# A two-layer decoder trunk on one core: values and gates in three passes, chunk products by fours, output gates in alternating banks, modulation transposes within a block, scores of 128 columns

## Chip, cores and metric

The kernel runs on one core of a Trainium2 chip. The time is the device time of one execution in microseconds (us), as the median of several runs. TensorE (PE) does the matrix products, VectorE (DVE) and ScalarE (ACT) the elementwise work, GpSimd (POOL) some fills and sums, and SyncE (SP) starts most of the transfers.

## The reference

1024 tokens of 1024 numbers, all in 32-bit floats, go through two layers. Layer 0 mixes tokens with an mLSTM of 8 heads (q and k 64 wide, v 128 wide, chunks of 128 tokens) and has a squared-ReLU MLP of 4096. Its result gives keys and values for causal attention with a low-rank latent and a rotary part in layer 1, which has an MLP as well. Around each part stand norms whose gains and shifts (the modulation) are computed from a condition vector by products with matrices of 1024 x 6144.

```python
proj = h @ w_in                       # 1024 x 3088: q 512, k 512, v 1024, i 8, f 8, og 1024
q, k, v, ig, fg, og = jnp.split(proj, splits, axis=-1)
# per chunk of 128 tokens and head; ib = input gate, bb = running sum of log sigmoid(forget gate)
log_d = bb[..., :, None] - bb[..., None, :] + ib[..., None, :]      # causal part only
m_t = jnp.maximum(bb + m, jnp.max(log_d, axis=-1))
s = (q @ k.T) * exp(log_d - m_t)                  # scores times decay
num = exp(bb + m - m_t) * (q @ C) + s @ v         # C: the state, 64 x 128 per head
h = num / jnp.maximum(jnp.abs(den), exp(-m_t))    # den: the same with a column of ones for v
C = decay * C + (w * k).T @ v
y = (rmsnorm(h) * jax.nn.sigmoid(og)) @ w_out
...
x = x + g1 * rmsnorm(y);  h = modulate(rmsnorm(x), sh2, sc2);  x = x + g2 * rmsnorm(sqrelu_mlp(h))
```

## The kernel before

**Products.** A 32-bit number is written as a rounded high part and a rounded rest (hi and lo). `mm3` (L230 to L234) computes one product as three rounded ones: lo by hi (L232), hi by lo (L233), hi by hi (L234). Weights come by `wload` (L204, L211 for the transfer): SP brings 768 or 1024 columns into one of four `raw` buffers, ScalarE rounds them to hi (L189), VectorE subtracts (L190) and gives lo. Both parts stand in `ws`, eight buffers. `prompt` gives such work priority over the rest.

**Banks.** Results lie in PSUM: two tiles `ps` of one bank (512 columns of 32 bits), two `pc` of one bank, and two `pm` of two banks each.

**Tokens** go through in two halves of 512, `hfs[0]` and `hfs[1]`. For each half the mLSTM part is written as generators, and each `yield` ends a step:

- `qk_in` (the second half) and `qk_pairs` (the first): q and k with features on the partitions, from 24 products of 512 columns for each group of 128 features.
- `gates_in` (L626): the 16 gate columns of `w_in` are loaded, split, and set into a weight of 128 columns per block of 128 inputs. 16 pairs of products of 512 columns (L642, L643) give the gates with the gates on the partitions, in a `ps` bank `gp`. `gates0` (L702 to L751) then makes the decay terms on 8 partitions by a chain on VectorE and ScalarE from L707 to L751; at its end stands `RM`, the maxima and weights that later products read. Twelve transposes (L756) give the same per token, in `gc`.
- `intra0` (L761), for each of four pairs of heads: the decay of two heads by two products each in a `pc` bank (L772 the mask, L775 reading `RM`) and four exponentials each (L779), eight score products of 64 rows in a `pm` tile (L787), the product of both (L792), and one product of `selW` with `RM` (L795) that scales q.
- `v_in` (L657): the values, with tokens on the partitions: four passes of 256 columns, each with two loads and for each block of 128 tokens 24 products of 256 columns, in a `ps` bank.
- `chunks0` (L814), for each chunk of 128 tokens: q with the state `Cst` (L831, 64 rows), the weighted scores `PT` with v (L836, 128 rows), transposes of k (L844), the new state (L879) and transposes of the result (L894), which are written over `PT`.
- `og0` (L690): the output gates, eight projections in `ps`, each with three activations (L695 to L697). `split_o` multiplies and splits them for `wout`, the projection after.

**Background.** `ada_chunk` (L348) computes the modulation: four transfers of two 512-column blocks into `raw` (L353), eight products on VectorE (L358, L360) that sum them into `tma`, two empty steps, then four transposes (L340) into a `pc` bank and a reduction (L342). 24 such chunks of both layers stand in `bg0` and `bg1`.

**What sets the order.** The generators are put together by hand: `with_bg(g, bg, n)` takes n background steps with each step of g, `weave` and `weave_n` take so many steps of a second generator with each of the first, `in_turn` runs three side by side. A scheduler then places what they issue by its own costs and priorities; each engine runs its instructions in the order that results. In the MLPs and the attention, `two_streams` (L2028) runs a dense generator (an MLP or a projection, whose steps report `"hid"` or `"within"`) with another, and takes background steps (`fill`) between them.

**Attention scores** (`score_mm`, L1506): for a block of 128 queries, the keys up to its end in groups of up to 512 columns, five products each and a mask (L1522). A group is at least 256 columns wide, even where only 128 of them are causal.

Of the kernel before, what the change touches and what calls it, by code (L numbers as in the profile page):

```python
# [82 lines left out]
def kernel(  # L83
# [542 lines left out]
    def gates_in(hf):  # L626
        h = hf.h
        wg = raw(F32R).rearrange("p (a b) -> p a b", b=P)
        nc.gpsimd.memset(wg.bitcast(F32), 0.0)
        rg = tmp()  # L630
        rgv = rg[:, :128].rearrange("p (k n) -> p k n", n=16)
        nc.sync.dma_start(rgv, wcols(w_in, 2048, 16))
        for g in range(2):
            s = ts(g, 8)
            nc.scalar.copy(wg[:, :, 32 * g : 32 * g + 8], rgv[:, :, s])
            nc.vector.tensor_sub(
                wg[:, :, 64 + 32 * g : 72 + 32 * g], rgv[:, :, s],
                wg[:, :, 32 * g : 32 * g + 8].bitcast(F32),
            )
        gp = ps()  # L640
        for k in range(KD):
            nc.tensor.matmul(gp, wg[:, k], h.lo[k], start=k == 0, stop=False)  # L642
            nc.tensor.matmul(gp, wg[:, k], h.hi[k], start=False, stop=k == KD - 1)  # L643
        hf.gp = gp
        yield from gates0(hf)
        yield
# [10 lines left out]
    def v_in(hf):  # L657
# [9 lines left out]
        for j in range(4):  # L667
            w0 = wload([(0, 0, wcols(w_in, 1024 + j * 256, 256, 0, 4))], 256)
            w1 = wload([(0, 0, wcols(w_in, 1024 + j * 256, 256, 4, 4))], 256)
            for t in range(4):  # L670
                pt = ps()[:, :256]
                for k in range(KD):
                    w = w0 if k < 4 else w1
                    mm3(
                        pt, h.hi[k][:, ts(t, P)], h.lo[k][:, ts(t, P)],
                        w[0][:, k % 4], w[1][:, k % 4], k == 0, k == KD - 1,
                    )
                i = pt.rearrange("p (a b) -> p a b", b=P)
                if j < 3:
                    parts = [(hf.v[t][8][:, 2 * j : 2 * j + 2, 0:128], i)]  # L680
                else:
                    parts = [(hf.v[t][6 + e][:, 0:128], i[:, e]) for e in range(2)]
                for o, a in parts:
                    if t % 2:
                        nc.vector.tensor_copy(o, a)
                    else:
                        nc.scalar.copy(o, a)
                yield
# [13 lines left out]
    def gates0(hf):  # L702
# [4 lines left out]
        nc.vector.tensor_copy(t1, gp[64:72])  # L707
        nc.vector.scalar_tensor_tensor(t1, gp[0:8], col(GB, 1)[0:8], t1, ALU.add, ALU.add)
        nc.vector.tensor_copy(t2, gp[96:104])
        nc.vector.tensor_copy(t3, gp[32:40])  # L710
        nc.vector.scalar_tensor_tensor(t2, t3, col(GB + 1, 1)[0:8], t2, ALU.add, ALU.add)
# [49 lines left out]
    def intra0(hf):  # L761
# [3 lines left out]
        for p_ in range(4):  # L765
# [18 lines left out]
            st = pm()  # L784
            for j in range(4):
                for r in range(2):
                    nc.tensor.matmul(  # L787
                        st[:, r, ts(j, P)], kp[ts(r, 64), ts(j, P)], qp[ts(r, 64), ts(j, P)],
                        start=True, stop=True,
                    )  # L790
            for r in range(2):
                nc.vector.tensor_mul(PT[:, r], st[:, r], E[r])  # L792
# [21 lines left out]
    def chunks0(hf):  # L814
# [4 lines left out]
        for j in range(4):  # L819
# [3 lines left out]
            nvs = []  # L823
            for q in range(2):
                num = pm()
                nv = num[:, :, 0 : 2 * VE].rearrange("p b (i e) -> p b i e", e=VE)
                for i in range(2):
                    p_ = 2 * q + i

                    for r in range(2 if g > 0 else 0):  # L830
# [1405 lines left out]
```

## Time and profile before

| | |
|---|---|
| median of 3 runs | 2370.01 us (2367.67 to 2371.02) |
| profiled execution | 2373.3 us, of which 2371.2 are the span from the first to the last instruction |
| TensorE busy | 2334.8 us, 98% of the span, 12197 products |
| weight loads of TensorE | 1967.3 us, 83%, beside the products |
| VectorE busy | 1605.2 us, 68% |
| ScalarE busy | 1099.8 us, 46% |
| GpSimd busy | 147.6 us, 6% |
| granted TensorE clock | 0.996 on average |
| transfers | 420.77 MB, 177 GB/s on average |

Stages by the timeline: the first half's values and intra products from 82 to 160 us, its chunks to about 225, the second half's projections, gates, intra products and values to about 326, its chunks to about 400, the second output gates to about 447. Attention scores stand between 972 and 1826 us, beside dense work.

How to read the lines: a timeline's row has the start in us, the duration, the engine, the line of the kernel, the operation, what it writes and reads, rows x columns of the weight tile, the shape, and in brackets the wait before it with what released it. A group's row has busy time and mean duration in ns behind the first bar, and the engine's idle time ahead of these instructions with its releasers behind the second. A window's row has the window's length and, for PE, the weight loads, VectorE, ScalarE and GpSimd, the busy time and number of instructions, then the granted clock, the busy share of the transfer engines and GB/s. Products overlap in a pipeline, so their durations add up to more than the time that passes.

### The profile page before, as it was taken

To read this page: it belongs to the slowest core of one execution; us is meant where nothing else is said; L and a number is where in the kernel's file an instruction comes from. 1 tells how busy PE (TensorE), PEld (TensorE's weight loads), DVE (VectorE), ACT (ScalarE), POOL (GpSimd) and SP (SyncE) were. 2 spreads that over 40 slices of the span, in tenths; PEclk is the share of its full clock that TensorE was granted. 3 is DMA by queue.
4 is the path that set the end of the run, shared out by engine and by line. 5 is a ranking of instruction groups with operands and counts; after the bars stand their busy time and mean duration, and the time that the engine had idled before them with its cause. 6 is when DMAs were issued, how large, how long until landed. Compare 5 with 4: busy or idle time off the path is not lost.

```text
span 2371.2 us, 32533 instructions
## 1 busy us (share of the span) xinstructions
PE 2334.8 (98%) x12197; PEld 1967.3 (83%) x12197; DVE 1605.2 (68%) x2657; ACT 1099.8 (46%) x1826; POOL 147.6 (6%) x345
## 2 busy tenths in 40 slices
PE   7999999999999999999999999999999999999998
PEld 5888888788888888888888888888888888989997
DVE  6667866868666677877774967766566478457556
ACT  4355334655333464434444544434434445655543
POOL 1000000000001210111110110001001000000000
PEclk9999999999999999999999999999999999999999
DMA  9453564544656966667754675885544552657552
GB/s 312 143 145 89 181 184 137 170 130 150 187 178 166 313 184 197 185 200 205 227 157 117 196 208 176 269 272 167 173 129 132 147 169 86 189 175 218 165 183 89
DMA packets 408350, 420.77 MB, mean 177 GB/s; under 512 B 27427, under 2 KB 310112, under 8 KB 404608
## 3 DMA queue, kind: packets, MB, share of 16 engines
q1 hardware_dynamic: 402272, 385.02, 51.9%
q0 software_dynamic: 5920, 33.66, 6.5%
q8 instruction: 96, 1.57, 0.3%
q14 instruction: 62, 0.51, 0.1%
HBM read 359.37 MB, written 92.80 MB: 191 GB/s over the span
## 4 chain that ended last, share of the span: by engine, by line
PE 90%; DVE 4%; DMA 3%; ACT 2%; issue 1%; SPq 0%; DVEq 0%; ACTq 0%
PE ps L232 16%; PE ps L233 15%; PE ps L234 15%; PE pm L232 10%; PE pm L233 10%; PE pm L234 10%; PE pc L234 2%; PE pc L232 2%; PE pc L233 2%; DMA raw<-in_mlp_w_dram 1%; PE pc L1637 1%; DMA raw<-in_a_w_in_dram 1%; DVE wl L190 1%; PE pm L836 1%; PE pm L1523 1%
## 5 line engine op out<-in xcount | busy, mean ns | idle before, releaser
L190 DVE TENSOR_TENSOR wl<-raw,wh 128x1024 fp32r<-128x1024 f32 (+2 forms) x382 | 458.5, 1203 | 385.8 <-ACT wh L189 281.4
L189 ACT CAST wh<-raw 128x1024 fp32r<-128x1024 f32 (+2 forms) x382 | 394.0, 1035 | 657.9 <-PE ps L232 241.8
L232 PE MATMUL ps<-k,wl 128*128 128x512 f32 (+1 forms) x1464 | 560.3, 383 | 2.6 <-ACT k L695 1.4
L234 PE MATMUL ps<-k,wh 128*128 128x512 f32 (+1 forms) x1464 | 551.6, 377 | 0.0
L233 PE MATMUL ps<-k,wh 128*128 128x512 f32 (+1 forms) x1464 | 550.7, 376 | 0.0
L232 PEld LDWEIGHTS ps<-k,wl 128*128 128x128 f32 x1464 | 275.7, 188 | 56.5 <-issue 3.6
L234 PEld LDWEIGHTS ps<-k,wh 128*128 128x128 f32 x1464 | 275.5, 188 | 51.7 <-issue 0.7
L233 PEld LDWEIGHTS ps<-k,wh 128*128 128x128 f32 x1464 | 275.9, 188 | 50.0 <-issue 1.9
L198 DVE TENSOR_TENSOR k<-k,pm 128x512 f32<-128x512 f32 (+1 forms) x254 | 211.2, 860 | 87.2 <-PE pm L234 86.1
L232 PE MATMUL pm<-hd,wl 128*128 128x512 f32 x512 | 201.1, 393 | 0.5 <-ACT hd L472 0.5
L233 PE MATMUL pm<-hd,wh 128*128 128x512 f32 x512 | 199.5, 390 | 0.2 <-DVE hd L473 0.2
L234 PE MATMUL pm<-hd,wh 128*128 128x512 f32 x512 | 199.4, 390 | 0.0
L232 PE MATMUL pm<-wh,hd 128*128 128x512 f32 x488 | 192.2, 394 | 3.9 <-ACT raw L1529 3.7
L233 PE MATMUL pm<-wl,hd 128*128 128x512 f32 x488 | 190.5, 390 | 0.0
L234 PE MATMUL pm<-wh,hd 128*128 128x512 f32 x488 | 190.3, 390 | 0.0
L360 DVE SCALAR_TENSOR_TENSOR tma<-raw,cond,tma 128x512 f32<-128x512 f32 x168 | 125.7, 748 | 20.0 <-DMA raw<-in_kv_ada_w_dram 13.8
L1529 ACT ACTIVATE raw<-pm,sm 128x128 f32<-128x128 f32 (+3 forms) x64 | 47.4, 741 | 155.1 <-DVE sm L1528 118.2
L473 DVE TENSOR_TENSOR hd<-tmp,hd 128x512 fp32r<-128x512 f32 x128 | 88.0, 689 | 40.4 <-ACT hd L472 39.8
L232 PEld LDWEIGHTS pm<-hd,wl 128*128 128x128 f32 x512 | 96.2, 188 | 20.9 <-ACT hd L472 0.9
L233 PEld LDWEIGHTS pm<-hd,wh 128*128 128x128 f32 x512 | 96.2, 188 | 20.5 <-DVE hd L473 0.5
L234 PEld LDWEIGHTS pm<-hd,wh 128*128 128x128 f32 x512 | 96.2, 188 | 20.2
L985 POOL COPY sm<-sm 128x1 f32<-128x1 f32 x128 | 51.9, 412 | 967.2 <-DVE sm L984 930.3
(385 smaller groups left out, 4064.1 us busy)
## 6 DMA issues: line engine op xcount, KB each, us to landing
raw<-in_mlp_w_dram SPq DMA_DIRECT2D x240, 512.0 KB, 4.3
raw<-in_ada_w_dram SPq DMA_DIRECT2D x80, 512.0 KB, 4.3
raw<-in_a_w_in_dram SPq DMA_DIRECT2D x48, 512.0 KB, 4.8
sums<-in_mlp_w_dram POOLq DMA_DIRECT2D x96, 256.0 KB, 4.8
raw<-sums SPq DMA_DIRECT2D x64, 256.0 KB, 3.7
xs<-k SPq DMA_DIRECT2D x40, 256.0 KB, 3.6
raw<-in_kv_ada_w_dram SPq DMA_DIRECT2D x16, 512.0 KB, 3.9
raw<-in_a_w_out_dram SPq DMA_DIRECT2D x16, 512.0 KB, 5.0
```

The source lines that it names most:

```text
L189: nc.scalar.copy(hi[:, :n], r[:, :n])
L190: i = nc.vector.tensor_sub(lo[:, :n], r[:, :n], hi[:, :n].bitcast(F32))
L198: return f(*a, **k)
L232: nc.tensor.matmul(o, ll, rh, start=start, stop=False, **m)
L233: nc.tensor.matmul(o, lh, rl, start=False, stop=False, **m)
L234: pe_last[0] = nc.tensor.matmul(o, lh, rh, start=False, stop=stop, **m)
L360: nc.vector.scalar_tensor_tensor(acc, r[:, kk], cond[:, k : k + 1], acc, ALU.mult, ALU.add)
L473: nc.vector.tensor_sub(lo, u, hi.bitcast(F32))
L836: nc.tensor.matmul(nv[:, r, i], hf.PT[p_][:, r, cs], v[2 * p_ + r], start=g == 0, stop=True,)
L985: now = nc.gpsimd.tensor_copy(seen, flag)
L1523: nc.tensor.matmul(o[:, :w], qh, kh, start=False, stop=True)
L1529: nc.scalar.activation(pr[:, :n], f, AF.Exp, bias=m, scale=SCALE, accum_out=l)
```

## The change

1. **Values and gates in three passes.** `v_in` computes heads 6 and 7 and the 16 gate columns (which stand right behind the values in `w_in`) in one pass of 272 columns, with three blocks of 128 inputs to a load, then heads 0 to 2 and 3 to 5 in passes of 384 columns, with two blocks to a load. Results are collected in the two `pm` tiles. The gates come out with tokens on the partitions, go into a zeroed tile `hf.graw`, and four transposes bring them onto 32 + 8 partitions in a `pc` bank. `gates0` loses the two copies that summed hi and lo parts. The order around it changes: in the first half six steps of the values stand first, then the rest of them woven with gates and intra products (background rate 0.73 instead of 1); in the second half the six steps come first as well, then q and k and the rest of the values with background rate 1.5 (1.7 before), and gates and intra products beside them.
2. **Chunk products by fours.** `chunks0` takes the head pairs of both `pm` tiles in turn: four products on 64 rows, then four on 128 rows.
3. **The scores of `intra0`** go into two `ps` banks instead of one `pm` tile.
4. **The second output gates** (`og0` of the second half) use a `ps` and a `pm` bank in turn.
5. **Modulation within a block:** `two_streams` takes its background steps after the first step that reports `"within"`, not after one that reports `"hid"`.
6. **Scores of 128 columns** where only 128 are causal.

```diff
     def gates_in(hf):
...
-        gp = ps()
-        for k in range(KD):
-            nc.tensor.matmul(gp, wg[:, k], h.lo[k], start=k == 0, stop=False)
-            nc.tensor.matmul(gp, wg[:, k], h.hi[k], start=False, stop=k == KD - 1)
+        gp = pc()
+        for t in range(4):
+            nc.tensor.transpose(gp[0:64, ts(t, P)], hf.graw[:, t], ident)
...
     def v_in(hf):
...
-        for j in range(4):
-            w0 = wload([(0, 0, wcols(w_in, 1024 + j * 256, 256, 0, 4))], 256)
-            w1 = wload([(0, 0, wcols(w_in, 1024 + j * 256, 256, 4, 4))], 256)
-            for t in range(4):
-                pt = ps()[:, :256]
...
+        for h0, nh, kg in ((6, 2, 3), (0, 3, 2), (3, 3, 2)):
+            n = nh * P + (16 if h0 == 6 else 0)
+            b = [pm(), pm()]
+            for k0 in range(0, KD, kg):
+                nk = min(kg, KD - k0)
+                w = wload([(0, 0, wcols(w_in, 1024 + h0 * P, n, k0, nk))], n)
+                for t in range(4):
+                    for k in range(nk):
+                        kk = k0 + k
+                        mm3(
+                            b[t // 2][:, t % 2, :n], h.hi[kk][:, ts(t, P)], h.lo[kk][:, ts(t, P)],
+                            w[0][:, k], w[1][:, k], kk == 0, kk == KD - 1,
+                        )
...
-    def og0(hf, alloc):
+    def og0(hf, alloc, wide=False):
...
-            pt = proj_fm(w_in, 2064 + k * P, hf.h)
+            pt = proj_fm(w_in, 2064 + k * P, hf.h, (lambda: pm()[:, 0]) if wide and k % 2 else ps)
...
-            st = pm()
+            st = [ps(), ps()]
...
     def chunks0(hf):
...
+            for i in range(2):
+                for q, nv in enumerate(nvs if g > 0 else []):
                     p_ = 2 * q + i
-                    for r in range(2 if g > 0 else 0):
+                    for r in range(2):
                         nc.tensor.matmul(
                             nv[:, r, i], hf.q[p_ // 2][ts(r, 64), p_ % 2, cs],
                             Cst[ts(r, 64), p_], start=True, stop=False,
                         )
+                for q, nv in enumerate(nvs):
+                    p_ = 2 * q + i
                     for r in range(2):
                         nc.tensor.matmul(
                             nv[:, r, i], hf.PT[p_][:, r, cs], v[2 * p_ + r],
                             start=g == 0, stop=True,
                         )
...
-            w = max(256, min(512, n - g * 512))
+            w = min(512, n - g * 512)
...
-    drain(with_bg(gates_in(hfs[0]), bgs, 1))
+    main = with_bg(v_in(hfs[0]), bgs, 0.73)
+    for _ in range(6):
+        next(main)
     x1 = load_x1()
-    drain(weave(with_bg(v_in(hfs[0]), bgs, 1), intra0(hfs[0]), 1.5))
+    drain(weave(main, chain(gates_in(hfs[0]), intra0(hfs[0])), 1.5))
...
-    drain(gates_in(hfs[1]))
-    main = chain(twice(qk_in(hfs[1])), v_in(hfs[1]))
-    for _ in range(4):
-        next(main)
-    drain(split_o(hfs[0]))
-    for _ in range(2):
-        next(main)
-    drain(weave_n(with_bg(main, bgs, 1.7), intra0(hfs[1]), 0.8))
+    v1 = v_in(hfs[1])
+    for n in range(6):
+        next(v1)
+        if n == 4:
+            drain(split_o(hfs[0]))
+    main = chain(twice(qk_in(hfs[1])), v1)
+    drain(weave_n(with_bg(main, bgs, 1.5), chain(gates_in(hfs[1]), intra0(hfs[1])), 0.8))
...
-    for k, _ in enumerate(og0(hfs[1], k4v)):
+    for k, _ in enumerate(og0(hfs[1], k4v, True)):
...
-                at[0] = go(dense)
+                was, at[0] = at[0], go(dense)
...
-                if at[0] == "hid":
+                if at[0] == "within" and was == "hid":
                     some(fill, per)
```

Line numbers of the changed kernel are smaller by 5 in the middle of the file: its gate transposes are L629, L756 becomes L751, L772 and L775 become L767 and L770, L831 and L836 become L826 and L833.

**Where the instructions move: TensorE at the second half's gates.** Before, the order runs from the gate products (L642, L643, into `ps_2169`) over 118 products of 512 columns of the projections to the twelve transposes L756 and the first product that reads `RM`, L775.

```order
L642 MATMUL ps_2169<-k_233_1433,raw_2161 128x512
L232 MATMUL ps_2252<-k_226_1426,wl_2249 128x512
...
L756 MATMUL pc_2228<-ident,tmc_2186 128x8
L232 MATMUL ps_2372<-k_228_1428,wl_2369 128x512
...
L772 MATMUL pc_2414<-identb,maskA 128x512
L775 MATMUL pc_2414<-RM,e_116 128x512
```

Now the gates come from `graw` (`tmp_2057`) by L629, and 43 products of 512 columns (19 into `ps_2304`, 24 into `ps_2363`) stand between those transposes and L751.

```order
L233 MATMUL ps_2304<-k_227_1313,wh_2300 128x512
L629 MATMUL pc_2253<-ident,tmp_2057 64x128 x4
L234 MATMUL ps_2304<-k_226_1312,wh_2300 128x512
...
L234 MATMUL ps_2363<-k_232_1318,wh_2359 128x512
L751 MATMUL pc_2330<-ident,tmc_2258 128x8
L340 MATMUL pc_2344<-ident,tma_1257 128x128 x4
...
L770 MATMUL pc_2396<-RM,e_116 128x512
L767 MATMUL pc_2443<-identb,maskA 128x512
L770 MATMUL pc_2443<-RM,e_116 128x512
L232 MATMUL ps_2417<-k_226_1312,wl_2414 128x512
```

What moved: the projections that stood between the gates and the readers of `RM` now stand partly ahead of the gates, and the next projection (`ps_2417`) is queued behind four products of the decay.

**TensorE at a chunk.** Before, the products of a chunk of the first half alternate by twos between 64 rows (L831, with `Cst`) and 128 rows (L836).

```order
L831 MATMUL pm_1823<-Cst,k_79_373 128x130 x2
L836 MATMUL pm_1823<-k_129_745,hd_791 128x130 x2
L544 MATMUL ps_1785<-ident,k_124_733 128x128 x2
L544 MATMUL ps_1785<-ident,k_125_734 128x128 x2
L831 MATMUL pm_1823<-Cst,k_79_373 128x130 x2
L836 MATMUL pm_1823<-k_129_745,hd_909 128x130 x2
```

Now those of a chunk go by fours, over both `pm` tiles.

```order
L826 MATMUL pm_3396<-Cst,k_393_2209 128x130 x2
L826 MATMUL pm_3397<-Cst,k_394_2210 128x130 x2
L833 MATMUL pm_3396<-k_371_2053,hd_2393 128x130 x2
L833 MATMUL pm_3397<-k_371_2053,hd_2722 128x130 x2
L826 MATMUL pm_3396<-Cst,k_393_2209 128x130 x2
L826 MATMUL pm_3397<-Cst,k_394_2210 128x130 x2
```

What moved: two runs of each kind have become one that is twice as long.

**SP at the second half's values.** Before, a pass of values has two weight loads of 4 x 256 columns (L211), and four loads of the modulation (L353) follow.

```order
L211 DMA raw_2653<-in_a_w_in_dram 128x4x256
L211 DMA raw_2659<-in_a_w_in_dram 128x4x256
L353 DMA raw_2692<-in_ada_w_dram 128x2x512
L353 DMA raw_2696<-in_ada_w_dram 128x2x512
L353 DMA raw_2726<-in_ada_w_dram 128x2x512
```

Now the loads of values are 2 x 384 columns each, one at a time, with those of the modulation between.

```order
L211 DMA raw_2831<-in_a_w_in_dram 128x2x384
L353 DMA raw_2852<-in_ada_w_dram 128x2x512
L353 DMA raw_2874<-in_ada_w_dram 128x2x512
L353 DMA raw_2878<-in_ada_w_dram 128x2x512
L211 DMA raw_2894<-in_a_w_in_dram 128x2x384
L353 DMA raw_2912<-in_ada_w_dram 128x2x512
```

What moved: loads of values and of the modulation, which take the same four `raw` buffers, now alternate singly or in twos and threes.

More of the change, by code (lines that the diff above doesn't have):

```diff
@@ L666, in v_in @@
             hf.v[t].append(v)
-        for j in range(4):
-            w0 = wload([(0, 0, wcols(w_in, 1024 + j * 256, 256, 0, 4))], 256)
-            w1 = wload([(0, 0, wcols(w_in, 1024 + j * 256, 256, 4, 4))], 256)
-            for t in range(4):
-                pt = ps()[:, :256]
[L672 to L683, printed above, removed]
-                    if t % 2:
[L685 to L688, printed above, removed]
@@ L822, in chunks0 @@
             v = hf.v[j]
[L823 to L827, printed above, removed]
+            nums = [pm(), pm()]
+            nvs = [
+                num[:, :, 0 : 2 * VE].rearrange("p b (i e) -> p b i e", e=VE) for num in nums
+            ]
+            for i in range(2):
+                for q, nv in enumerate(nvs if g > 0 else []):
                     p_ = 2 * q + i
-                    for r in range(2 if g > 0 else 0):
+                    for r in range(2):
                         nc.tensor.matmul(
@@ L2032, in two_streams @@
         at, per = ["hid"], 0
+        was = "hid"
         while True:
```

43 lines of the change are left out of this document (23 added, 20 removed).

## Prediction

> **What bounds the kernel now.** I read the page's engine totals, the span in slices and the chain that ended last; then TensorE's groups by shape; then the timeline, for the distance from one product's start to the next.
>
> ```profile
> span 2371.2 us, 32533 instructions
> PE 2334.8 (98%) x12197; PEld 1967.3 (83%) x12197; DVE 1605.2 (68%) x2657; ACT 1099.8 (46%) x1826; POOL 147.6 (6%) x345
> PE   7999999999999999999999999999999999999998
> PEclk9999999999999999999999999999999999999999
> PE 90%; DVE 4%; DMA 3%; ACT 2%; issue 1%; SPq 0%; DVEq 0%; ACTq 0%
> ```
>
> TensorE is busy in every slice but the first at full clock, and 90% of the chain is its own work. So the time is the sum of the distances between products plus a few waits, and an instruction elsewhere costs something only where TensorE waits for it. The mean durations are no price, since products overlap; the distances are:
>
> ```profile
> 1001.23 0.39 PE L234 MATMUL pm<-hd,wh 128*128 128x512 f32 x1
> 1001.23 0.19 PEld L232 LDWEIGHTS pm<-hd,wl 128*128 128x128 f32 x1
> 1001.46 0.40 PE L232 MATMUL pm<-hd,wl 128*128 128x512 f32 x1
> ...
> 1060.86 0.34 PE L1518 MATMUL pm<-k,k 128*128 128x384 f32 x1
> 1061.04 0.33 PE L1519 MATMUL pm<-hd,k 128*128 128x384 f32 x1
> 1061.21 0.34 PE L1520 MATMUL pm<-hd,k 128*128 128x384 f32 x1
> ...
> 144.01 0.28 PE L232 MATMUL ps<-wh,k 128*128 128x256 f32 x1
> 144.13 0.28 PE L233 MATMUL ps<-wl,k 128*128 128x256 f32 x1
> ```
>
> A product of 512 columns takes 0.23 us of TensorE, one of 384 takes 0.175, one of 256 takes 0.12 (a duration of 0.40 is that plus the pipeline). On a line through the last two, 272 columns take 0.127.
>
> **The change, part by part.** All prices are us of TensorE; below zero is a gain.
>
> ```profile
> L642 PE MATMUL ps<-k,raw 128*128 128x512 f32 x16 | 6.3, 397 | 0.0
> L643 PE MATMUL ps<-k,raw 128*128 128x512 f32 x16 | 6.4, 397 | 0.0
> L232 PE MATMUL ps<-wh,k 128*128 128x256 f32 x288 | 82.7, 288 | 0.8 <-DVE k L685 0.8
> 161.18 1.04 PE L894 MATMUL pc<-ident,tmc 128*128 128x128 f32 x8
> 162.15 0.49 PE L831 MATMUL pm<-Cst,k 64*128 64x130 f32 x2
> ```
>
> Gates: 32 products of 512 columns go, 32 x 0.23 = 7.3. Eight transposes come; eight in a row take 0.97 here (161.18 to 162.15), and they stand in three places with another tile size, so 1.0 (0.5 to 2.5). Net -6.3. The small load, casts, and fills that go with them lay beside TensorE's work and count zero.
>
> Values: 768 products of 256 columns (256 of each line, of the 288 in the L232 row; the rest belong to the shared values) cost 92.2. They become 192 of 272 and 384 of 384: 24.4 + 67.2 = 91.6. Net -0.6 (to +0.5, if 384 columns take 0.178). The 0.8 of waiting for value copies in that row goes too, since whole banks now take turns: -1.4 together. Six more weight splits come, with no more columns; their cover is TensorE's product stream.
>
> ```profile
> 164.21 0.49 PE L831 MATMUL pm<-Cst,k 64*128 64x130 f32 x4
> 164.64 0.71 PE L836 MATMUL pm<-k,hd 128*128 128x130 f32 x4
> 165.28 0.49 PE L831 MATMUL pm<-Cst,k 64*128 64x130 f32 x4
> ...
> 120.82 0.72 PE L787 MATMUL pm<-k,k 64*128 64x128 f32 x8
> 121.46 0.51 PE L795 MATMUL pc<-RM,selW 128*128 128x512 f32 x1
> ```
>
> Chunk products: four records on 64 rows take 0.43, eight take 0.64. So a run twice as long saves 2 x 0.43 - 0.64 = 0.22: the price is the change between 64 and 128 rows, about 0.2 a run. By the order of the instructions the 64-row runs (L831) fall from 31 to 19 and the 128-row runs (L836) from 31 to 17; the first chunk of the second half keeps its old order. 26 x 0.2 = -5.2 (-6 to 0). The Trainium skill (TensorE: Matmul & The Clock Gate, Part 3, The mechanism) says that a weight load overlaps running products only when its row group differs. By that rule alternating is the cheap order and the fours gain nothing; the sum would be 5.2 higher. This trace disagrees: the weight load at 1001.23 runs, on the same 128 rows, under the product begun at 1001.23, while the changes of row count are where time is lost. The score products of 64 rows (L787), now in two single banks, are cut into 18 runs instead of 15: +0.6.
>
> ```profile
> L1518 PE MATMUL pm<-k,k 128*128 128x256 f32 x32 | 9.2, 288 | 0.0
> 972.72 0.23 PE L1522 MATMUL pm<-maskA,identb 128*128 128x128 bf16 x1
> 972.76 0.37 PE L1523 MATMUL pm<-k,k 128*128 128x256 f32 x1
> ```
>
> Narrow scores: half of the 32 products on each of five lines, 80 in all, go from 256 to 128 columns. No row shows a rounded 32-bit product so narrow. Nearest below is the bf16 mask, 0.04 (972.72 to 972.76), nearest above an unrounded product of 130 columns, two records of the 0.64 for four at 164.64 without the changes: 0.22. Between lies the 128-column transpose with a fresh weight each, 0.12 at 161.18 and 0.11 within its run; like it, the product loads 128 columns of 32-bit weights and passes once, so I take 0.11: -0.9 (-6.4 to +8.0).
>
> ```profile
> 435.23 0.50 PE L232 MATMUL ps<-k,wl 128*128 128x512 f32 x1 [1.37 <-ACT k L695]
> L233 PE MATMUL ps<-hd,k 128*128 128x256 f32 x160 | 46.6, 292 | 1.7 <-DVE hd L473 1.7
> L340 PE MATMUL pc<-ident,tma 128*128 128x128 f32 x96 | 14.8, 273 | 1.1 <-DVE tma L360 1.1
> ```
>
> Second output gates: the product at 435.23 waits for the sigmoid of an earlier bank; with banks in turn it goes, -1.4. Modulation transposes: L340 waits 1.1 on all 96, and not in the attention stretch, so their own waits give nothing. Moving them re-deals VectorE's order around the three waits of L233 on L473 (1.7 in all); I take -1.0 (-1.7 to +1).
>
> TensorE's part: -6.3 - 1.4 - 5.2 + 0.6 - 0.9 - 1.4 - 1.0 = -15.6.
>
> Now the waits that it adds. The gates' chain:
>
> ```profile
> 83.53 0.39 PE L643 MATMUL ps<-k,raw 128*128 128x512 f32 x1
> 83.96 0.69 DVE L707 COPY tmc<-ps 8x512 f32<-8x512 f32 x1 [1.77 <-PE ps L643]
> 100.94 0.68 DVE L751 TENSOR_TENSOR RM<-tmc,tmc 8x512 fp32r<-8x512 f32 x1
> ...
> 225.47 0.68 DVE L707 COPY tmc<-ps 8x512 f32<-8x512 f32 x1
> 246.19 0.69 DVE L342 TENSOR_REDUCE sm<-pc 128x4 f32<-128x512 f32 x1
> 246.80 0.48 DVE L358 TENSOR_SCALAR tma<-raw,cond 128x512 f32<-128x512 f32 x1
> 247.74 0.68 DVE L751 TENSOR_TENSOR RM<-tmc,tmc 8x512 fp32r<-8x512 f32 x1
> ```
>
> From the end of the gate product to RM, VectorE and ScalarE need 17.7 (83.92 to 101.62), and 23 in the second half, where splits stand between. In the second half of the new order TensorE has, from the gate transposes to the first product that reads RM, 43 products of 512 columns and little else: 43 x 0.23 + 0.5 = 10.4. The chain loses two copies, 1.4, and shares VectorE there with a reduction and two background products, some 1.9 by 246.19 and 246.80: 17.7 - 1.4 + 1.9 = 18.2. TensorE takes its instructions in order, so it stands 7.8, with the products of the next projection queued behind; their weight split comes after the chain on VectorE, one more of 1.2. Together +9 (5 where nothing shares VectorE, 10.5 where splits do).
>
> ```profile
> 262.00:340.00 78.00, 77.00 (x558) 70.29 (x557) 61.21 (x111) 25.66 (x54) 0.00 (x0) 1.00 0.76 229
> L190 DVE TENSOR_TENSOR wl<-raw,wh 128x768 fp32r<-128x768 f32 x8 | 7.6, 954 | 2.2 <-ACT wh L189 2.2
> L360 DVE SCALAR_TENSOR_TENSOR tma<-raw,cond,tma 128x512 f32<-128x512 f32 x168 | 125.7, 748 | 20.0 <-DMA raw<-in_kv_ada_w_dram 13.8 <-DMA raw<-in_ada_w_dram 4.2
> ```
>
> Second values: in this stretch VectorE is busy 61.2 of 78 (78%), and DMA at its busiest, 0.76. SP's order shows the new mix: a weight load of 768 columns feeds 24 x 0.175 = 4.2 of TensorE, and ten background loads go with six of them (0.40 a us; before four with two, which fed 11.5: 0.35), each freeing its one of four raw buffers only after two products of 0.75. With the intra products closer together VectorE comes near 90%, and each new weight waits for a raw buffer behind background work instead of coming in pairs. Eight weight loads, each late by none to one weight split plus a little (1.2): 0 to 9.6. I take +6, nearer the upper end, since a load has one load's cover instead of two.
>
> ```profile
> 116.73 0.38 PE L772 MATMUL pc<-identb,maskA 128*128 128x512 bf16 x1 [0.54 <-ACT tmc L779]
> L779 ACT ACTIVATE tmc<-pc,gc x64: 356/368/418, 104.6 to 318.1; 128x128 f32<-128x128 f32 x64
> ```
>
> First half: the intra products come faster too; six of eight decay products now stand within 8 us of TensorE's work, and each needs four exponentials of 0.37 and one of two banks. Six waits like 116.73 give 3.2, and the first chunk then waits for the last product of VectorE with no value products left to cover it. The loads of the second half's tokens also stand behind six value loads on SP. +4.5 (0 to 7).
>
> The sum: -15.6 + 9 + 6 + 4.5 = +3.9. The profiled execution took 2373.3 with its 2.1 around the span, so 2377.2; it stands 3.3 above the median of 2370.0, so as a median 2374.
>
> **Rivals.** Faster: the second gates' chain is covered. Speaking for it, the first half's new order leaves about 18 of products there and the old second half lost only 0.4. The point that decides is 18 of cover in the second half, against the 10.4 counted. Without that wait, and with value loads on time, -15.6 + 4.5 = -11: 2359.
>
> Slower by narrow scores: below 256 columns the product is run as the unrounded one, 0.22. Nothing here excludes it. Then +3.9 + 8.9 = +13: 2383.
>
> Slower by the value stretch: raw buffers, not VectorE, set the pace, and each of eight loads lands one background pair late, 8 x 1.5 = 12 instead of 6, and the second half's chunks start with it; with the first half at its end of 7, +12.4: 2382.
>
> Slower by the skill's rule: the fours give nothing, +9.1: 2379. The rows above speak against it.
>
> **Chances.** My forecast 0.60, that is -5 to +9 by its bounds; the faster rival 0.17; narrow scores 0.10; value stretch 0.10; the rule 0.03. About 0.2%, 4.7 us, is what a measurement of this kernel tells from no change. Of my forecast 0.39 lies within it, 0.19 above, 0.02 below. So faster 0.19, same 0.39, slower 0.42. My own range is 2365 to 2379; to leave out no more than 2 in 10, 2361 to 2385.
>
> **What would show it.** After: L643 gone; TensorE idle 7 to 10 before the products that read RM in the second half, released by VectorE and ScalarE; waits of value products (now in pm, 384 columns) on weight splits in the stretch before the second chunks; runs of eight 64-row records; 128-column scores 0.11 apart; no wait on L695's successor. The prediction is wrong if the second gates pass without a wait, or the narrow scores stand 0.22 apart.

## The result: 2410 us, slower by 1.7%

The changed kernel takes 2410.18 us (median of 4 runs, 2406.26 to 2413.67) against 2370.32 us for the kernel before: a ratio of 1.0166, 95% interval 1.0153 to 1.0178. Forecast were 2374 us and a range of 2361 to 2385; no rival reached past 2383. The change does not cost 4 us but 40. One execution of a later kernel, e8, ran at a mean granted clock of 0.556 and took 3880.64 us; the figures for e8 below leave it out.

The page of the changed kernel, engine totals, the clock's row and the chain that ended last:

```profile
span 2409.9 us, 32121 instructions
PE 2344.2 (97%) x11981; PEld 1971.7 (82%) x11981; DVE 1600.6 (66%) x2655; ACT 1098.1 (46%) x1824; POOL 147.6 (6%) x345
PEclk9999999999999999999999999999999999999999
PE 80%; DMA 9%; DVE 7%; ACT 2%; issue 2%; SPq 0%; DVEq 0%; ACTq 0%
```

There are 216 products fewer, and TensorE's own work fell from 90% of the chain to 80%: the time went into waits and, as shorter windows show, into a lower clock, of which the clock's row in 40 slices shows nothing. First the changed kernel (columns: stretch; length; PE, weight loads, DVE, ACT and POOL with their instructions; granted clock; DMA share; GB/s), then the nearest stretches of the kernel before (only in the attention do they hold nearly the same work, 1227 and 1224 products):

```profile
222.00:250.00 28.00, 25.91 (x146) 22.14 (x144) 21.49 (x42) 8.45 (x15) 0.00 (x0) 1.00 0.13 39
250.00:262.00 12.00, 7.58 (x25) 5.45 (x25) 11.06 (x17) 5.82 (x13) 0.00 (x0) 0.57 0.55 160
318.00:345.00 27.00, 22.82 (x116) 20.43 (x116) 19.47 (x33) 6.67 (x14) 0.00 (x0) 0.94 0.69 217
620.00:700.00 80.00, 73.89 (x323) 60.13 (x322) 47.92 (x60) 28.21 (x37) 0.00 (x0) 0.97 0.57 170
990.00:1250.00 260.00, 244.66 (x1227) 205.15 (x1227) 186.22 (x351) 99.47 (x187) 31.16 (x69) 0.96 0.61 178
```

```profile
250.00:326.00 76.00, 75.00 (x555) 68.01 (x555) 58.67 (x96) 25.89 (x57) 0.00 (x0) 1.00 0.76 234
612.00:690.00 78.00, 78.00 (x351) 64.60 (x350) 48.04 (x60) 26.71 (x36) 0.00 (x0) 1.00 0.61 183
972.00:1209.00 237.00, 234.44 (x1224) 197.54 (x1225) 182.02 (x347) 99.65 (x187) 30.80 (x69) 1.00 0.67 191
```

Three stretches lose. By the starts of the same products in both traces, the lag over the kernel before goes from -1.2 to +13.7 in the second half's gates and values, from +10.0 to +18.7 in the first MLP, and from +19.3 to +41.0 in the first attention; it ends at +37.4. From the second half's chunks to the output gates it falls by 3.7, and in the second attention by 3.5; elsewhere it hardly moves. In the attention 260 us stand for 237: idle time grew from 2.6 to 15.3, and 4% of 260 is another 10.4 at a lower clock, together the 23. In the MLP it is 6.1 of idle and, up to 700 us, 2.4 of clock. In the gates and values idle is 10.7 (2.1, 4.4 and 4.2), and the clock takes 0.43 x 12 + 0.06 x 27 = 6.8. So the clock takes 6.8 + 2.4 + 10.4 = 19.6 of the 40 us.

### The profile page after: what moved, and what is told of

Read it like the earlier page. It is cut to its first block, busy times and chain, and to the rows that moved or that the text cites. A ratio compares the mean times of both kernels' runs of the same rounds, so it can differ in the third digit from the quotient of the medians.

```text
span 2409.9 us, 32121 instructions
## 1 busy us (share of the span) xinstructions
PE 2344.2 (97%) x11981; PEld 1971.7 (82%) x11981; DVE 1600.6 (66%) x2655; ACT 1098.1 (46%) x1824; POOL 147.6 (6%) x345
## 4 chain that ended last, share of the span: by engine, by line
PE 80%; DMA 9%; DVE 7%; ACT 2%; issue 2%; SPq 0%; DVEq 0%; ACTq 0%
PE ps L232 13%; PE ps L233 12%; PE ps L234 12%; PE pm L232 10%; PE pm L233 9%; PE pm L234 9%; DMA raw<-in_mlp_w_dram 5%; DMA raw<-in_a_w_in_dram 2%; PE pc L234 2%; PE pc L233 2%; PE pc L232 2%; DVE wl L190 2%; ACT wh L189 1%; DVE tma L360 1%; PE pc L1633 1%
## 5 line engine op out<-in xcount | busy, mean ns | idle before, releaser
L190 DVE TENSOR_TENSOR wl<-raw,wh 128x1024 fp32r<-128x1024 f32 (+2 forms) x388 | 460.0, 1187 | 416.1 <-ACT wh L189 320.9
L189 ACT CAST wh<-raw 128x1024 fp32r<-128x1024 f32 (+2 forms) x388 | 395.7, 1022 | 717.0 <-PE ps L232 224.9
L232 PE MATMUL ps<-k,wl 128*128 128x512 f32 (+1 forms) x1432 | 549.3, 384 | 2.8 <-ACT tmp L1129 1.9
L234 PE MATMUL ps<-k,wh 128*128 128x512 f32 (+1 forms) x1432 | 541.6, 378 | 0.0
L233 PE MATMUL ps<-k,wh 128*128 128x512 f32 (+1 forms) x1432 | 540.7, 378 | 0.0
L234 PEld LDWEIGHTS ps<-k,wh 128*128 128x128 f32 x1432 | 271.3, 189 | 50.5 <-issue 0.5
L233 PEld LDWEIGHTS ps<-k,wh 128*128 128x128 f32 x1432 | 271.5, 190 | 49.2 <-issue 1.7
L198 DVE TENSOR_TENSOR k<-k,pm 128x512 f32<-128x512 f32 (+1 forms) x254 | 211.1, 859 | 82.2 <-PE pm L234 81.0
L233 PE MATMUL pm<-hd,wh 128*128 128x512 f32 x512 | 199.4, 390 | 0.2 <-DVE hd L473 0.2
L233 PE MATMUL pm<-wl,hd 128*128 128x512 f32 x488 | 190.3, 390 | 0.0
L360 DVE SCALAR_TENSOR_TENSOR tma<-raw,cond,tma 128x512 f32<-128x512 f32 x168 | 125.7, 748 | 34.7 <-DMA raw<-in_ada_w_dram 16.8
L473 DVE TENSOR_TENSOR hd<-tmp,hd 128x512 fp32r<-128x512 f32 x128 | 88.0, 688 | 41.4 <-ACT hd L472 40.8
L233 PEld LDWEIGHTS pm<-hd,wh 128*128 128x128 f32 x512 | 96.1, 188 | 20.5 <-DVE hd L473 0.5
```

The lines of the kernel that those rows point to most:

```text
L189: nc.scalar.copy(hi[:, :n], r[:, :n])
L190: i = nc.vector.tensor_sub(lo[:, :n], r[:, :n], hi[:, :n].bitcast(F32))
L198: return f(*a, **k)
L232: nc.tensor.matmul(o, ll, rh, start=start, stop=False, **m)
L233: nc.tensor.matmul(o, lh, rl, start=False, stop=False, **m)
L234: pe_last[0] = nc.tensor.matmul(o, lh, rh, start=False, stop=stop, **m)
```

## The price of a wait

The changed kernel in the first attention: the last product ahead of the wait ends by 1065.8, the scores' banks come late, and the products behind stand farther apart (0.43 in place of 0.227 for 512 columns):

```profile
1069.19 1.22 DVE L198 TENSOR_TENSOR k<-k,pm 128x1024 f32<-128x1024 f32 x1
...
1070.46 0.33 PE L1513 MATMUL pm<-k,k 128*128 128x128 f32 x1 [4.71 <-DVE sm L980]
...
1075.77 0.63 PE L233 MATMUL ps<-k,wh 128*128 128x512 f32 x1
1076.20 0.63 PE L234 MATMUL ps<-k,wh 128*128 128x512 f32 x1
```

The profile names L980 as what ended the wait, a fill of one column that this product does not read; L198, which reads the scores' bank `pm` out, ends at the same time, 1070.41. The windows around it:

```profile
1065.40:1070.40 5.00, 0.36 (x2) 0.00 (x0) 4.93 (x10) 0.00 (x0) 0.00 (x0) 1.00 0.00 1
1070.80:1077.60 6.80, 6.80 (x29) 6.13 (x29) 4.87 (x17) 1.52 (x7) 1.23 (x3) 0.50 0.73 186
1077.60:1084.00 6.40, 6.40 (x34) 5.37 (x33) 3.17 (x6) 3.31 (x7) 0.76 (x3) 1.00 0.06 5
```

A wait of 4.7 us is followed by 6.8 us at half clock: 3.4 us are lost on top. The same 0.50 follows the gates' wait, for 10.2 us. The forecast priced every wait at its length.

## Experiments

**e1: part 5 alone** (the background's place in two_streams).

```diff
-                at[0] = go(dense)
+                was, at[0] = at[0], go(dense)
...
-                if at[0] == "hid":
+                if at[0] == "within" and was == "hid":
                     some(fill, per)
```

> The kernel before with one part of the change alone: background steps of the two streams are taken after the first report of 'within' that follows 'hid'. Between the traces of before and after, TensorE falls behind by another 22 us from 1025 to 1210 us, in waits of score products (L1513) for VectorE. Theory A, the place of the background steps makes them: this kernel takes 2370 + 22 to 26 = 2392 to 2396 us, with waits of 4 to 5 us before the score products of the first attention. Theory B, the narrow scores made them (each score group is ready sooner and so asks sooner for its banks): no difference, 2370 us.

Measured: 2386.29 us against 2370.45, ratio 1.0062 (1.0047 to 1.0077). Theory A in kind, a third smaller: the lag grows by 15 us between 990 and 1210. Theory B falls, since the scores here are 256 wide.

**e2: part 6 alone.**

```diff
-            w = max(256, min(512, n - g * 512))
+            w = min(512, n - g * 512)
```

> The kernel before with scores of 128 columns alone; the order of all other instructions stays. Theory A: between the traces TensorE wins 3.6 us in the second attention, where nothing else changed, and there are as many narrow products in the first attention, so -4 to -6, 2364 to 2366 us. Theory B (the narrow scores made the new waits of the first attention): 2370 + 20 = 2390 us.

Measured: 2370.93 against 2370.45, ratio 1.000 (0.999 to 1.0009). Neither number: the medians show no gain that can be told. Theory B falls. Its profiled execution is 2.9 us shorter; by the lags it gains 0.6 in the first attention and 2.0 in the second. But e1 and e5, whose scores are 256 wide, gain 3.2 and 2.7 in the second attention as well: there the trace of the kernel before ran at half clock for 3.4 us, and theirs did not.

```profile
1580.20:1583.60 3.40, 3.40 (x12) 2.86 (x11) 0.86 (x2) 0.00 (x0) 0.00 (x0) 0.50 1.04 425
```

So the 3.6 us of Theory A were read from a place where the kernel before had lost time, and are not the narrow scores'.

**e3: values, gates and their order alone**, parts 1 and 3 of the diff above on the kernel before.

> The kernel before with values and gates in three passes, their order, and the score products of intra0 in single banks; chunk products, output gates, background place and score width as before. Theory A: this part carries the +16 between the first half's chunks and the second half's, and the +8.7 in the first MLP as well (620 to 700 us, waits of the modulation transposes L340), since it moves the background on by a step and the order of VectorE and SP changes there: 2370 + 22 to 25 = 2392 to 2395 us. Theory B, the waits in the first MLP come from the output gates or the background's place: 2370 + 13 to 16 = 2383 to 2386 us.

Measured: 2395.26, ratio 1.0098 (1.0077 to 1.0119): Theory A. Its lag is -0.3 at the end of the first half, +15.9 at the second half's chunks, +18.2 behind the output gates, +25.0 behind the first MLP, and stays.

**e4: all but part 5**, the changed kernel with e1's line put back.

> The changed kernel with the background steps at their old place, all else changed. Theory A (place of the background): 2410 - 22 to 26 = 2384 to 2388 us, without waits over 2 us before the score products of the first attention. Theory B (narrow scores): 2410 us, the same waits.

Measured: 2388.69, ratio 1.0078 (1.0061 to 1.0095): Theory A, 0.7 us above its numbers. Part 5 costs 21.5 us in place, 15.8 alone.

**e5: one background step more in the kernel before.**

```diff
+    next(bgs)
     for k, _ in enumerate(og0(hfs[1], k4v)):
```

> The kernel before with one more step of the background taken ahead of the second output gates; nothing else changed. The changed kernel enters the first MLP with one background step more taken (64 against 63 ahead of that place). Theory A, the phase of the background against the MLP's blocks makes the waits of the modulation transposes (L340 for L360, 2 to 4 us each, between 600 and 700 us): the same waits come here, +6 to +7, 2376 to 2377 us. Theory B, they come from something else in the values part: 2370 us.

Measured: 2379.29, ratio 1.0033 (1.0024 to 1.0043), +8.6; by the lags 2.4 at the output gates and 6.0 in the first MLP. Theory A: one step moved suffices, with nothing of the change itself. Here are the waits of the transposes L340 (group's releasers with us and times) in the kernel before, the changed one and e5, and e5's wait. A row adds the waits of the weight loads to those of the products; the products alone wait 1.1 us in the kernel before, 0.6 + 3.4 + 2.2 in the changed one and 4.3 in e5.

```profile
  DVE tma L360: 2.6, 2
```

```profile
  DVE tma L360: 13.5, 6
```

```profile
  DVE tma L360: 9.1, 2
```

```profile
642.46 1.11 PE L340 MATMUL pc<-ident,tma 128*128 128x128 f32 x4 [4.34 <-DVE tma L360]
```

The background steps by fours at the MLP's blocks, so a step more moves the transposes of a chunk to an earlier block (571.19 us in e5, 579.51 in the kernel before). In the kernel before, the transposes of successive chunks stand 22.3 us apart on TensorE, two blocks of the MLP (579.51, 601.76, 624.00), while the first products of successive chunks on VectorE stand 23.8 apart (629.70, 653.53, 677.45): the background runs late a little more with each chunk, and a block less of slack turns into waits.

**e6: cover ahead of the gates' transposes** in e4.

```diff
+        pt = pc()
+        for n in range(36 if half else 0):
+            nc.tensor.matmul(pt, hf.h.hi[0][:, 0:P], hf.h.hi[n % KD], start=True, stop=True)
...
```

> All parts but the background's place (2388.7 us), with 36 products of 512 columns that nobody reads set ahead of the second half's gate transposes (L751), 36 x 0.227 = 8.2 us of TensorE work about as long as the wait there; the output stays as it was. In the trace without them TensorE runs at half clock for 10.2 us after that wait. Theory A, the clock after a wait costs by itself: the wait's 8 us become 8 us of work, the half clock goes, so 2388.7 - 5 = 2384 us, and no granted clock under 1 between 250 and 270 us. Theory B, a wait costs its length alone: 2389 us.

Measured: 2392.88, ratio 1.0086 (1.0070 to 1.0101). The interval takes in Theory B's 2389, but the trace shows neither theory. From 222 us on, e4 (53 us) and e6 (58 us, with 20 products more besides the 36):

```profile
222.00:275.00 53.00, 46.40 (x233) 37.83 (x232) 40.33 (x75) 17.35 (x33) 0.00 (x0) 0.90 0.33 100
```

```profile
222.00:280.00 58.00, 55.02 (x289) 45.62 (x289) 43.74 (x79) 19.77 (x39) 0.00 (x0) 0.97 0.34 101
```

The clock's loss falls from 5.3 to 1.7 and idle from 6.6 to 3.0, 7.2 in all, for 8.2 of work put in. The last wait stays, 2.45 us, with a spell at half clock from 264.2 us: on ScalarE the next weight's cast (260.95 us) stands behind an evacuation (L202, 259.96) that waits for TensorE, which the cover holds back, and then waits 0.40 us for its transfer; which of the two alone would have held it is not shown. Work in a wait pays only if nothing that ends the wait depends on it. This trace also lost some 3 us in the first half, at a spell at 148 us, where nothing was changed.

**e7: parts 2, 4 and 6** of the diff above on the kernel before.

> The kernel before with chunk products by fours, alternating banks of the second output gates, and scores of 128 columns; values, gates and background as before. Theory A: fours -3.1 (the two traces of before and after draw apart by 1.0 in the first half's chunks and 2.1 in the second's), output gates -1.6, narrow scores -2.4: 2370.3 - 7 = 2363 us. Theory B, that a weight load overlaps only a product with another row group, so fours give nothing: 2366 us.

Measured: 2362.06 (5 runs), ratio 0.9964 (0.9951 to 0.9976), -8.6: faster than both kernels. By the lags the fours give 4.5 and the output gates 1.75; waits and one spell at half clock at the first attention's start take 2.7 back. The second attention gains 3.1, of which e5 has 2.7 without narrow scores (see e2), so little of it is theirs. Part of one chunk before and in e7:

```profile
181.77 0.49 PE L831 MATMUL pm<-Cst,k 64*128 64x130 f32 x4
182.19 0.72 PE L836 MATMUL pm<-k,hd 128*128 128x130 f32 x4
...
183.27 0.49 PE L831 MATMUL pm<-Cst,k 64*128 64x130 f32 x4
183.70 0.71 PE L836 MATMUL pm<-k,hd 128*128 128x130 f32 x4
```

```profile
180.98 0.72 PE L831 MATMUL pm<-Cst,k 64*128 64x130 f32 x8
...
182.12 1.06 PE L838 MATMUL pm<-k,hd 128*128 128x130 f32 x8
```

**e8: the second half's gates earlier**, on e4, and **e11: the same kernel again.**

```diff
...
+        next(g1)
+        yield from twice(qk_in(hfs[1]))
+        yield from v1
+    main = with_bg(second(), bgs, 1.24)
+    for _ in range(12):
+        next(main)
+    drain(weave_n(main, chain(g1, intra0(hfs[1])), 0.9))
```

> All parts but the background's place (2388.7 us), with the second half's gates started behind the first pass of values, six steps of projections behind them before any intra product, and the background spread over all 38 steps at 1.24 (47 steps in place of 48, so that the first MLP is entered as in the kernel before). Theory A: the gate wait goes with its half clock (8 + 5), the waits of the first MLP go (6.9), so 2388.7 - 20 = 2369 us. Theory B: the value stretch is bound by VectorE and raw buffers and gives the gate wait back there: 2380 us or more.

> The kernel of e8 once more, for a profile at full clock: 2374 us. If the gate wait is gone and the first MLP waits too, TensorE is ahead of e4 by 13 us at the second half's chunks and by 14 to 20 us behind the first MLP; what is left over the 2369 that was expected stands in the value stretch from 280 to 340 us.

Measured: 2373.59 (9 runs), ratio 1.0013 (1.0004 to 1.0022); e11 2375.51 (a single run). The gates' wait is gone, and 14 to 15 of the 20 us came back: by the lags e11 is ahead of e4 by 7.0 at the second half's chunks, where 13 were expected, and by 14.2 behind the first MLP. The rest stands elsewhere than expected, ahead of the value stretch:

```profile
238.38 0.50 PE L232 MATMUL ps<-k,wl 128*128 128x512 f32 x1 [2.86 <-DVE wl L190]
...
258.76 0.50 PE L232 MATMUL ps<-k,wl 128*128 128x512 f32 x1 [3.09 <-DVE wl L190]
...
276.70 1.36 PE L782 MATMUL ps<-k,k 64*128 64x128 f32 x8 [2.23 <-ACT k L198]
```

```profile
256.40 1.04 ACT L189 CAST wh<-raw 128x1024 fp32r<-128x1024 f32 x1 [5.70 <-DMA raw<-in_a_w_in_dram]
```

Weights come late: the casts L189 ahead of these three places waited 4.14, 5.70 (the last row) and 3.77 us for their transfers. Ahead of the first split two instructions of the gates' chain and one background product stand on VectorE as well. And the first MLP still waits once (2.6 us, then half clock, by the lags 3.1 in all).

**e9: cover in the first attention** of the changed kernel.

```diff
+            pt, kh = pc(), cover
+            for _ in range(15):
+                nc.tensor.matmul(pt, kh[:, 0:P], kh, start=True, stop=True)
         us = begin()
```

> The changed kernel (2410 us) with 15 products of 512 columns that nobody reads in front of the first score products of the second, third and fourth pair of the first attention, where TensorE stood 4.7, 3.6 and 3.8 us and then ran 6.8 us at half clock each time. Their 15 x 0.227 = 3.4 us fit into each wait, whose end VectorE sets; the output stays as it was. Theory A, the half clock after a wait is a cost of its own: 3 x 3.4 = 10 us go, 2400 us, and the granted clock stays at 1.0 there. Theory B, only the wait's length counts: 2410 us.

Measured: 2406.82, ratio 1.0146 (1.0125 to 1.0167); the interval overlaps that of the changed kernel. Against the runs of the kernel before beside it (2372.07) it is slower by 34.8, the changed kernel by 39.9. The trace is clearer, timeline and window:

```profile
1063.86 3.56 PE L1672 MATMUL pc<-k 128*128 128x512 f32 x15
1067.57 0.33 PE L1513 MATMUL pm<-k,k 128*128 128x128 f32 x1
1067.73 0.27 PE L1514 MATMUL pm<-k,k 128*128 128x128 f32 x1
1067.84 0.27 PE L1515 MATMUL pm<-hd,k 128*128 128x128 f32 x1
```

```profile
990.00:1240.00 250.00, 245.70 (x1267) 205.03 (x1268) 183.96 (x349) 99.13 (x187) 31.60 (x69) 1.00 0.63 185
```

With 45 products more the first attention is 8.0 us shorter by the lags, and the clock stays at 1.00. That the half clock costs by itself is shown there; its size over whole runs is not settled to better than some us.

**e10, e12: other queues for the transfers**, on e1.

```diff
-            nc.sync.dma_start(r, wcols(w, c0, 512, 2 * q, 2))
+            (nc.gpsimd if late[0] and buf is raw else nc.sync).dma_start(r, wcols(w, c0, 512, 2 * q, 2))
...
-                nc.sync.dma_start(kd[2 * p_ + r, i, :, ts(hf.i, H)], kn[r][i].bitcast(F32))
+                (nc.sync if hf.i else nc.gpsimd).dma_start(kd[2 * p_ + r, i, :, ts(hf.i, H)], kn[r][i].bitcast(F32))
```

The first line is both kernels', the second (and the same for `vd`) e12's alone.

> The background's new place alone (2386.3 us), with the background's transfers in the first attention issued by POOL in place of SP, so that no weight load of the MLP stands behind a background load that waits for a raw buffer; TensorE's order is the same. Theory A, SP's order makes the weights late (VectorE waits 4.0 us for one before the scores at 1049.7 us): the waits before the scores go, 2371 to 2374 us. Theory B, the background's products stand on VectorE ahead of the evacuations that the scores wait for, whoever issues the transfers: 2386 us with the same waits.

> The background's new place alone (2386.3 us), with the background's transfers and the stores of keys and values of the first attention issued by POOL, so that SP's queue has nothing that waits ahead of the MLP's weight loads but the weights' own buffers. Theory A, SP's order makes the weight late that VectorE then waits 4.0 us for: that wait goes and the waits before the scores with it, 2371 to 2374 us. Theory B, the weight waits for its turn in the four raw buffers behind the background's loads: the weight is issued as late as before, 2386 us or more.

Measured: e10 2393.46 (1.0086, 1.0071 to 1.0101) and e12 2384.63 (1.0065, 1.0048 to 1.0082). The waits before the scores stay (2.8, 1.2 and 3.0 us in e12, 3.1, 3.5 and 3.3 in e1), so SP's order is not the cause. SP in e1, then in e12, where only weight loads are left (the row joins two issues, the first at 1032.97):

```profile
1021.82 1.24 SPq L353 DMA_DIRECT2D raw<-in_ada_w_dram  x2
...
1030.21 0.38 SPq L353 DMA_DIRECT2D raw<-in_ada_w_dram  x1
...
1033.34 0.56 SPq L211 DMA_DIRECT2D raw<-in_mlp_w_dram  x1
```

```profile
1032.97 15.69 SPq L211 DMA_DIRECT2D raw<-in_mlp_w_dram  x2
```

The weight is issued at the same moment: it waits for a raw buffer, which the weight split before it frees (L190, from 1031.66 to 1032.89 in e1). The three others hold background blocks from 1022 to 1030 on, and VectorE first reads one at 1045.16 (e1):

```profile
1041.13 1.23 DVE L190 TENSOR_TENSOR wl<-raw,wh 128x1024 fp32r<-128x1024 f32 x1 [3.99 <-ACT wh L189]
...
1044.45 0.68 DVE L342 TENSOR_REDUCE sm<-pc 128x4 f32<-128x512 f32 x1
1045.16 0.49 DVE L358 TENSOR_SCALAR tma<-raw,cond 128x512 f32<-128x512 f32 x1
...
1045.68 1.54 DVE L360 SCALAR_TENSOR_TENSOR tma<-raw,cond,tma 128x512 f32<-128x512 f32 x2
...
1048.40 1.22 DVE L198 TENSOR_TENSOR k<-k,pm 128x1024 f32<-128x1024 f32 x1
```

L358 writes the one buffer `tma`, which the transposes of the chunk before read at 1040.28 in e1 and at 1018.41 in the kernel before. So by the code this one buffer holds L358 back until then; for the 4 us after that L358 stands in VectorE's order behind the late split (L190). No run gave the background a second such buffer, so this part of the chain is argued and not shown.

**e13: half of the background's products** in the first attention, on e1.

```diff
-            for kk in range(2):
+            for kk in range(1 if light[0] and buf is raw else 2):
```

> The background's new place alone (2386.3 us), with half of the background's products on VectorE left out in the first attention (one of two blocks of each transfer, so its modulation is not the reference's); transfers, their order and the buffers as there. Between the late weight split and the evacuation that frees the scores' banks VectorE runs five background instructions, 4.5 us of its time, of which 1.5 to 2.3 go. Theory A, their time on VectorE makes the wait: each of three waits of 3.1 to 3.5 us shrinks by 1.5 to 2.3 and the half clock after them goes, 2386 - 8 to 12 = 2374 to 2378 us. Theory B, the late weight alone makes it: 2384 to 2386 us.

Measured: 2377.95, ratio 1.0033 (1.0021 to 1.0044), -8.3: Theory A's number. At the three waits before the scores it is 1.5 to 1.7 us from product to product, where it was 3.5 to 3.9, and no half clock follows. The first wait in e1, then the same in e13:

```profile
1049.67 0.58 PE L1517 MATMUL pm<-k,k 128*128 128x256 f32 x1 [3.08 <-DVE sm L984]
```

```profile
1038.46 1.23 DVE L190 TENSOR_TENSOR wl<-raw,wh 128x1024 fp32r<-128x1024 f32 x1 [2.83 <-ACT wh L189]
...
1046.33 0.39 PE L1519 MATMUL pm<-k,k 128*128 128x256 f32 x1 [1.26 <-DVE sm L986]
```

But its mechanism is the smaller part. From the late split (L190) to the evacuation (L198) VectorE takes 6.6 us where it took 7.3, at all three waits, so the shorter run of products gives 0.7. The wait of that split for its weight falls by 1.2 to 1.6 (3.99 to 2.83 at the first): the weight too comes sooner, although only VectorE's products were cut. Of the 4.5 us that the text above gives the background there, the rows of e1 show 3.6 (L342, L358, L343 and three L360 ahead of L198). Of the 15.8 us of e1, 7.6 stay.

## Why the prediction was wrong

Its sum was +3.9; measured +39.9. Two things failed: a term that was taken for a small gain and was the largest loss, and the price of a wait. Step by step:

- **Modulation transposes, "-1.0 (-1.7 to +1)": the step that failed.** It cost 15.8 alone and 21.5 in place. The text looked at the waits that were there (L340, L233 on L473) and asked which would go. It did not follow what the moved step holds: three raw buffers, one `tma`, and 3.6 us of VectorE directly ahead of the evacuation (L198) that the scores need. There VectorE waited 4.0 to 4.4 us for a weight and TensorE 3.1 to 3.5 us for the scores' banks, at three places of e1. The order of the changed kernel's VectorE showed that place.
- **Every wait was priced at its length.** The sum has no term for the clock, which took 19.6 us at the three places; e9 shows that this loss is a cost of its own.
- **No term for the first MLP.** The rates 0.73 and 1.5 in place of 1 and 1.7 were read as load on the value stretch; that they leave the background one step further on at the MLP's start was not counted. e3 shows +6.8 there, e5 +6.0 from the step alone.
- **Gates and values of the second half, +9 and +6:** the waits came where they were put, L770 behind VectorE and ScalarE, value products behind weight splits, and were shorter, 9.5 of idle more than before against 15. The half clock added 6.8. That is 16.3; the stretch grew by 14.9 although some 4 of work went, so 2 to 3 more are lost in short steps that these rows do not show one by one.

```profile
236.42 0.60 PE L629 MATMUL pc<-ident,tmp 128*64 128x128 f32 x4
...
251.09 0.22 PE L751 MATMUL pc<-ident,tmc 8*128 8x8 f32 x1 [2.39 <-ACT tmc L736]
252.69 1.23 PE L751 MATMUL pc<-ident,tmc 8*128 8x8 f32 x10 [1.38 <-ACT tmc L738]
255.01 0.79 PE L770 MATMUL pc<-RM,e 128*128 128x512 f32 x1 [1.09 <-DVE RM L746]
```

- **First half, +4.5 against savings:** the balance is right, e3 ends it at -0.3 and the changed kernel at -1.2; the waits are so only in part. TensorE's idle time from 82 us to the first half's end is 3.0 us against 1.4 before: 1.56 stand ahead of the first chunk, as said, but only 0.39 at the decay products, where six waits of 3.2 were counted. What else ate the savings these rows do not show.
- **Chunk products, -5.2:** right, 4.5. Theory B of e7, by which the fours give nothing, falls. It came from the rule on row groups of the Trainium skill (TensorE: Matmul & The Clock Gate, Part 3, The mechanism), with which this trace does not agree: the weight load at 1001.23 us runs under a product on the same 128 rows.
- **Output gates, -1.4:** right, 1.75. **Narrow scores:** 0.11 us apart, as taken (1067.73 and 1067.84 in e9); the rival of 0.22 falls. Their gain is too small for the medians to tell, as -0.9 would be.

So the terms on TensorE's own work held, and the error lies in what moved work makes others wait for, and in a wait's price. That the sum was above zero is in part luck: the second half's gates and values, on which it rested, lost 14.9 of the 39.9 us, and what lost more it took for a gain or left out.

## What to carry to other kernels

Price a wait of TensorE of some 2 us or more at its length plus half of the spell at half clock behind it, and look for that in short windows: of 35 such waits in these traces, their starts and ends left out, 29 had one. When background work moves, follow its buffers: which ring it fills, when they are read out, and what stands behind its products on VectorE; and count its steps, since one step more can turn slack into waits hundreds of us on. Separate a bundle: three of these six parts gave 8.6 us, and the others cost over 45.

## What was not expected of the hardware

The spells at half clock inside the traces last 3.41, 6.83 or 10.24 us, and once, in e3, 13.65. In the changed kernel those after 250 us, the kernel's last one left out, start at 251.62, 333.54, 650.97, 698.76, 1070.81, 1149.32 and 1227.83 us, which is 24, 93, 14, 109, 23 and 23 times 3.413 us apart. The length of a wait does not decide alone: one of 2.17 us (at 698 us in the changed kernel) had a spell, those of 2.15 (at 1172 us in e12) and 3.09 (at 258.76 us in e11, above) had none, and in e7 two stops of 0.65 and 0.79 us (at 964 and 967 us) had one. The Trainium skill (TensorE: Matmul & The Clock Gate, Part 1, What's actually happening) gives free-running windows of about 3.4 us, of which an idle one halves the clock and a busy one restores it. The lengths and the distances agree; that a stop shorter than a window sufficed does not follow from it.
